# The context's columns of the second block's projection, computed in the two mixtures of experts; a scheduling fence ahead of the recurrence

## The chip, the cores and the metric

One core of a Trainium2 chip runs the whole network in one launch. The metric is the device time of one execution in microseconds (us), taken as the median of several runs. The engines are PE (matrix products), DVE and POOL (elementwise), ACT (activations, copies) and SP (which only starts transfers); ACT and POOL start transfers too. Each engine works off a queue of its own in order.

## The reference

1024 tokens of width 1024 pass two layers, each an attention mixer and a mixture of 16 experts; then a second block takes them together with 256 context tokens `ctx`. In each mixture an expert chooses its 128 best tokens over the whole sequence, so no expert can begin before the scores of all tokens are ranked.

```python
def ec_moe(h, w_router, w_gate, w_up, w_down):
    aff = jax.nn.softmax(jnp.einsum('bsd,de->bse', h, w_router), axis=-1)
    gates, idx = lax.top_k(aff.transpose(0, 2, 1), cap)
    xs = jax.vmap(lambda hb, ib: hb[ib])(h, idx)
    ...
def trunk_layer(x, xc, ...):                      # the second block; xc = ctx
    h = modulate(rmsnorm_2(x, norm1_g), shift1, scale1)
    hc = modulate(rmsnorm_2(xc, norm1_g), modc[0], modc[1])
    q, k, v, rw, gl = jnp.split(h @ w_in, IN_SPLITS, axis=-1)
    qc, kc, vc, rwc, glc = jnp.split(hc @ w_in, IN_SPLITS, axis=-1)
    ya = latent_window_attention(q, k, v, kc, vc, sink)
    ... short_conv(rw), short_conv(rwc), the recurrence over the context's tokens, then over x's
```

Of the context's row of `w_in` only 1952 columns are wanted: keys and values (256) and what the recurrence takes (1696). They depend on `ctx`, `c_ctx` and weights alone, not on the layers before.

## The kernel before

The work runs in stages: even attention with its output projection, mixture 1, odd attention with its output projection, mixture 2, norms and projection of the second block, the recurrence (with the gates' products and the window attention as fill), the merge and the last dense layer. A list scheduler of the language fixes, when the program is built, the order of each engine's queue from the order of the code, priorities and its own idea of durations; at run time an engine never passes its next instruction. Buffers come from rings: `raw` (8) holds loaded weight blocks, `ring` (4 in the mixtures) their two parts.

A float32 product is made of three: each operand is split into a high part (ACT, line 111) and the rest (line 116, on DVE or POOL), `w_h`, `w_l` and `xH`, `xL`, and `passes` lists the three products. In a mixture (`Moe`), the output projection's sink `add` normalises each token tile, `rank` keeps every expert's best (DVE, one `MAX8` and one `MATCH_REPLACE8` after the other), and `choose` ends in `thrb` (lines 682 to 686), the threshold that PE transposes. `gather` then counts places (`oh`), and POOL fetches an expert's tokens (`xs<-h_d,idx`). `gate_up` multiplies them by the expert's first four blocks (48 products of 512 columns); the scheduler has put the splits of expert 0's four blocks ahead of the choice, their low parts on POOL. After an expert POOL adds its tokens to `x_d` (line 805).

In the second block `block2_norms` makes `hH`, `hL` of the tokens and `cH`, `cL` of the context. `Rwkv.project` takes one tile of 128 features after the other through `conv`: two groups of 24 products of 512 columns for the tokens, one of 24 products of 256 columns for the context (`proj_feat`), then the short convolution on DVE. `Window.project` stands between them piece by piece; its tiles 8 and 9 are the context's. Then `R.open` clears tiles and loads constants, and the recurrence's groups take their operands `AR`, `BKf` from DRAM; `others` is the fill (`wK`, `wQ` of the window attention, `ghH`, `ghL`, `gw` of the gates).

Of the kernel before, what the change touches and what calls it, by code (L numbers as in the profile page):

```python
# [23 lines left out]
F32 = mybir.dt.float32  # L24
F32R = mybir.dt.float32r
# [18 lines left out]
class K:  # L44
    """Engines, pools and the few operations that every phase uses."""
# [31 lines left out]
    def banks(s, es, **n):  # L77
        """The eight banks of PSUM, by what they are for, until es closes."""
# [29 lines left out]
    # float32 as the sum of two float32r parts, exact  # L108
# [9 lines left out]
    def row_max(s, pool, todo, mx):  # L118
        """Largest of scores + mask by rows, one column of mx each."""
# [5 lines left out]
    def to_rows(s, pool, cols, n, *dst):  # L125
        """The negatives of columns, one after the other in rows of partition 64."""
# [13 lines left out]
    def weights(s, raw, ring, src, shape, leng=None, queue=None):  # L140
        """A block of weights, loaded and split."""
# [11 lines left out]
    def rstd(s, ss, n, scale, eps, name):  # L153
        """(ss * scale + eps) ** -0.5, few elements per partition."""
# [6 lines left out]
    def bcast(s, pool, ap, n, name, parts=128, **kw):  # L161
        """A row of n values in DRAM on every partition."""
# [5 lines left out]
    def norm_pair(s, pool, xs, gb, outs, eps=EPS, gb2=None):  # L168
        """Two token tiles normalised over their 1024 features and scaled by gb (plus gb2)."""
# [11 lines left out]
    def transpose4(s, src, n=4):  # L181
        """Four [128, 128] blocks of a token tile, transposed into one PSUM bank."""
# [5 lines left out]
    def to_hT(s, src, hH, hL, t):  # L188
        """A token tile [128, 1024] into features by tokens, split."""
# [12 lines left out]
# ---------------------------------------------------------------- even mixer  # L202
# [49 lines left out]
def proj_tile(k, hH, hL, W, t, n):  # L252
    """h of token tile t times a block of weights given in chunks of two k-tiles."""
# [113 lines left out]
NQ = 4  # heads whose operands are on chip at a time  # L367
# [31 lines left out]
def even_head(k, p2, mb, mc, me, h, slot, q_d, k_d, v_d, a_d, r_d):  # L399
# [13 lines left out]
    # values, by tokens shifted by half a tile and by residue classes of 4  # L413
# [2055 lines left out]
```

## Time and profile before

| what | us |
|---|---|
| runs (median of three) | 4460.52 |
| lowest and highest run | 4454.09, 4467.20 |
| span of the profiled execution (no other time of its own is given) | 4467.4 |
| PE busy, share of the span | 3963.4, 89% |
| DVE, ACT, POOL busy | 2938.6, 1815.5, 1109.1 |
| the two longest waits of PE together (line 686, the choice) | 60.2 |

Times in the rows are counted from the first instruction of the profiled execution. A row of the timeline gives start, duration, engine, line, operation, output and inputs, how many were merged, and in brackets how long the engine had been idle and what ended that. Busy shares are averages: PE is at 98% in one stage and at nothing in another.

### The profile page before, as it was taken

The numbers are of one execution on the slowest core, as the hardware profiler recorded it, in microseconds if no ns is written. First come the engines' busy times: TensorE is split into PE (matmuls) and PEld (weight loads), VectorE is DVE, ScalarE is ACT, GpSimd is POOL, SyncE is SP. The second block draws the span as 40 slices with busy tenths as digits, with TensorE's granted clock in tenths as the row PEclk, the third lists the DMA queues.
The fourth block names the chain that finished last, engine by engine and source line by source line (L and its number), as shares of the span: only waits on it lengthen the run. The fifth ranks groups of instructions, "written<-read, shape, count | busy, mean of one in ns | idle before, by whom it ended". The sixth has DMA issues, their size and how long they took to land. (4 is left out here: it accounts for less than half of the span.)

```text
span 4467.4 us, 65652 instructions
## 1 busy us (share of the span) xinstructions
PE 3963.4 (89%) x24208; PEld 3233.3 (72%) x24208; DVE 2938.6 (66%) x5925; ACT 1815.5 (41%) x3066; POOL 1109.1 (25%) x1069
## 2 busy tenths in 40 slices
PE   7898995897978999689948997999988899999998
PEld 7797884775855666567737776777777678888887
DVE  8656658896678875879866793766677565332334
ACT  3223332675447775257634452333333432212212
POOL 2211212121213433112133363222244511101101
PEclk9998997999989999889968998989998999999999
DMA  5758435898267543569933446555756662111112
GB/s 163 228 170 187 110 112 186 304 367 279 82 189 176 116 102 93 188 238 365 329 111 118 148 148 181 138 142 137 166 145 147 190 210 88 57 48 48 49 55 85
DMA packets 568286, 714.12 MB, mean 160 GB/s; under 512 B 243636, under 2 KB 355332, under 8 KB 567964
## 3 DMA queue, kind: packets, MB, share of 16 engines
q1 hardware_dynamic: 467788, 510.50, 37.3%
q0 software_dynamic: 42480, 144.62, 11.9%
q10 hardware_dynamic: 57696, 54.80, 3.8%
q8 instruction: 191, 3.13, 0.3%
q14 instruction: 131, 1.07, 0.1%
HBM read 555.84 MB, written 153.53 MB: 159 GB/s over the span
## 5 line engine op out<-in xcount | busy, mean ns | idle before, releaser
L116 DVE TENSOR_TENSOR w_l<-w_raw,w_h 128x2048 fp32r<-128x2048 f32 (+5 forms) x336 | 592.2, 1769 | 194.1 <-ACT w_h L111 192.9
L111 ACT ACTIVATE w_h<-w_raw 128x2048 fp32r<-128x2048 f32 (+4 forms) x344 | 507.2, 1487 | 437.4 <-PE psO L138 254.5
L138 PE MATMUL psA<-w_h,hH 128*128 128x256 f32 (+3 forms) x896 | 292.6, 330 | 28.9 <-ACT w_h L111 13.7
L138 PE MATMUL psA<-w_l,hH 128*128 128x256 f32 (+3 forms) x896 | 292.6, 327 | 1.9 <-DVE w_l L116 1.7
L138 PE MATMUL psA<-w_h,hL 128*128 128x256 f32 (+3 forms) x896 | 291.3, 326 | 0.0
L116 POOL TENSOR_TENSOR uL<-relu,uH 128x512 fp32r<-128x512 f32 x64 | 82.6, 1291 | 571.9 <-ACT uH L111 571.9
L138 PE MATMUL psA<-w_h,xH 128*128 128x512 f32 x512 | 208.5, 409 | 11.6 <-ACT xH L111 8.8
L138 PE MATMUL psA<-w_l,xH 128*128 128x512 f32 x512 | 211.1, 412 | 7.1 <-DVE w_l L116 6.9
L138 PE MATMUL psA<-w_h,xL 128*128 128x512 f32 x512 | 206.1, 404 | 4.3 <-DVE xL L116 4.3
L138 PEld LDWEIGHTS psA<-w_h,hH 128*128 128x128 f32 x896 | 174.5, 196 | 41.6 <-ACT w_h L111 15.1
L2287 DVE TENSOR_TENSOR relu<-relu 128x512 f32<-128x512 f32 x64 | 44.3, 693 | 238.2 <-ACT relu L2286 238.2
L116 DVE TENSOR_TENSOR PL<-P,PH 128x512 fp32r<-128x512 f32 x192 | 171.1, 903 | 27.3 <-ACT PH L111 27.1
L138 PEld LDWEIGHTS psA<-w_l,hH 128*128 128x128 f32 x896 | 175.3, 196 | 10.4 <-DVE w_l L116 4.6
L138 PE MATMUL psA<-ghH,gwH 128*128 128x256 f32 x512 | 169.6, 331 | 14.5 <-DMA ghH<-hs_d 5.0
L138 PEld LDWEIGHTS psA<-w_h,hL 128*128 128x128 f32 x896 | 175.1, 195 | 5.3 <-issue 2.6
L805 POOL DMA_INDIRECT x_d<-yo,idx x32 | 69.8, 2182 | 421.5 <-ACT yo L804 417.5
L111 ACT ACTIVATE gwH<-gw 128x256 fp32r<-128x256 f32 x256 | 103.3, 414 | 163.1 <-PE psA L138 121.0
L138 PE MATMUL psA<-ghH,gwL 128*128 128x256 f32 x512 | 161.2, 315 | 1.3 <-POOL gwL L116 1.0
L138 PE MATMUL psA<-ghL,gwH 128*128 128x256 f32 x512 | 160.4, 313 | 0.0
L116 POOL TENSOR_TENSOR gwL<-gw,gwH 128x256 fp32r<-128x256 f32 x128 | 97.5, 765 | 248.3 <-ACT gwH L111 207.5
L111 ACT ACTIVATE PH<-P 128x512 fp32r<-128x512 f32 x256 | 154.5, 629 | 6.5 <-POOL PL L116 1.3
L116 POOL TENSOR_TENSOR PL<-P,PH 128x512 fp32r<-128x512 f32 x64 | 90.9, 1420 | 231.2 <-ACT PH L111 178.2
(654 smaller groups left out, 11896.8 us busy)
## 6 DMA issues: line engine op xcount, KB each, us to landing
w_raw<-in_moe_w_gate_dram SPq DMA_DIRECT2D x64, 1024.0 KB
w_raw<-in_moe_w_up_dram SPq DMA_DIRECT2D x64, 1024.0 KB
w_raw<-in_moe_w_down_dram SPq DMA_DIRECT2D x64, 1024.0 KB
gw<-in_w_in_t_dram POOLq DMA_DIRECT2D x64, 512.0 KB, 5.5
wada<-in_w_ada_dram POOLq DMA_DIRECT2D x48, 512.0 KB, 5.8
w_raw<-in_w_mlp_up_dram SPq DMA_DIRECT2D x16, 1024.0 KB
w_raw<-in_w_mlp_down_dram SPq DMA_DIRECT2D x16, 1024.0 KB
AR<-ar_d SPq DMA_DIRECT2D x40, 256.0 KB
```

The source lines that it names most:

```text
L111: s.a.activation(h, x, AF.Copy)
L116: (eng or s.v).tensor_tensor(l, x, f(h), op=ALU.subtract)
L138: s.t.matmul(ps, a, b, start=first and i == 0, stop=last and i == n - 1)
L805: k.g.indirect_dma_start(out=s.x_d[:, :], out_offset=off, in_=y, in_offset=None, compute_op=ALU.add)
L2287: k.v.tensor_tensor(a, a, a, op=ALU.mult)
```

## The change

The context's normalised tokens are made during the even attention and kept in DRAM (`ctx_h`). Each mixture loads four blocks of `w_in` (two chunks of 512 columns), ahead of expert 0's, and `project` multiplies the 256 context tokens by them: 96 products of 512 columns, results to DRAM (`ctx_u`). The splits of expert 0's blocks are written behind that. The second block loads `ctx_u` as `cu` (2 MB), so that norms, splits and 384 products of 256 columns for the context go; `conv` turns a tile of `cu` with two transposes in their place, and the window's tiles 8 and 9 read `cu`. Ahead of `R.open` stands `no_sync_barrier()`, across which the scheduler moves no instruction; it makes nothing wait at run time. Comments and docstrings, which also change, are left out here.

```diff
@@ def even_mixer
     nc, tc = k.nc, k.tc
+    k.ctx = Context(k, w, mod_d)
@@ new class
+class Context:
+    LO, N = 512, 1952
+    CHUNKS = ((512, 1024), (1536, 1952))
...
+    def norms(s):
+        k, w = s.k, s.w
+        with ExitStack() as es:
+            p = k.pool(es, "Rctx", 1)
+            g, ga, x = (p.tile([128, D], F32, name=n) for n in ("cg", "ca", "cx"))
...
+            row(g, w["norm1_g_2"][0])
+            row(ga, s.mod_d[7])
+            k.v.scalar_tensor_tensor(ga, ga, 1.0, g, op0=ALU.add, op1=ALU.mult)
+            row(g, s.mod_d[6])
+            for t in range(2):
+                k.a.dma_start(x, w["ctx_2"][0, 128 * t:128 * t + 128])
+                k.norm_pair(p, [x], ga, [x], gb2=g)
+                k.a.dma_start(s.h_d[t], x)
+    def blocks(s, i):
+        return [s.w["w_in_t"][:, 4 * j:4 * j + 4, lo:lo + 512] for lo in s.CHUNKS[i] for j in range(2)]
+    def project(s, i, p, x, W):
+        k = s.k
+        for c, lo in enumerate(s.CHUNKS[i]):
+            for t in range(2):
+                ps = k.psA()
+                pairs = []
+                for j in range(2):
+                    wh, wl = W[2 * c + j]
+                    for q in range(4):
+                        pairs += passes(x[t][0][:, 4 * j + q], x[t][1][:, 4 * j + q], wh[:, q], wl[:, q])
+                k.mm(ps, pairs)
+                o = p.tile([128, 512], F32, name="th")
+                k.a.activation(o, ps, AF.Copy)
+                a = 2048 - lo if lo == 1952 else 0
+                k.a.dma_start(s.u_d[t][:, lo + a - s.LO:lo + 512 - s.LO], o[:, a:])
@@ class Moe
+        if i == 0:
+            k.ctx.norms()
...
-            split = [k.weights(raw, ring, x, [128, 4, 512], leng=k.g) for x in blocks[:4]]
-            del blocks[:4]
+            first = [k.weights(raw, ring, x, [128, 4, 512], leng=k.g) for x in k.ctx.blocks(i)]
+            split = []
...
-            s.choose()
...
+            def context(t):
+                xs = p.tile([128, D], F32, name="xs", bufs=3)
+                k.d.dma_start(xs, k.ctx.h_d[t])
+                return turned(xs)
+            x = [context(t) for t in range(2)]
+            s.choose()
...
             todo = [s.gather(p, e) for e in range(3)]
+            k.ctx.project(i, p, x, first)
+            split += [k.weights(raw, ring, x, [128, 4, 512], leng=k.g) for x in blocks[:4]]
+            del blocks[:4]
             gu = gate_up(turned(todo[0][0]))
@@ the second block
-        cH = hp.tile([128, 8, TC], F32R, name="cH")
-        cL = hp.tile([128, 8, TC], F32R, name="cL")
+        cu = hp.tile([128, 2, Context.N], F32, name="cu")
+        k.g.dma_start(cu, k.ctx.u_d.rearrange("t p c -> p t c"))
...
             k.banks(es1, Q=1, L0=1, L1=1, P0=1, P1=1)
+            k.tc.no_sync_barrier()
             R.open(es1)
@@ def block2_norms
-        ca = k.bcast(p1, mod_d[7], D, "ca")
-        cs = k.bcast(p1, mod_d[6], D, "cs")
-        k.v.scalar_tensor_tensor(ca, ca, 1.0, g, op0=ALU.add, op1=ALU.mult)
...
-        k.norm_pair(p, xs, ca, xs, gb2=cs)
-        for t in range(2):
-            k.to_hT(xs[t], cH, cL, t)
@@ Window.project
-                ps = proj_tile(k, hH, hL, W, t, 256) if t < 8 else proj_tile(k, cH, cL, W, t - 8, 256)
-                o = p2.tile([128, 256], F32, name="qo")
-                k.a.activation(o, ps, AF.Copy)
+                if t < 8:
+                    ps = proj_tile(k, hH, hL, W, t, 256)
+                    o = p2.tile([128, 256], F32, name="qo")
+                    k.a.activation(o, ps, AF.Copy)
+                else:
+                    o = cu[:, t - 8, 0:256]
@@ Rwkv.project, conv
-                ps = proj_feat(k, cH, cL, W, off, m, slice(0, TC))
+                ps = k.psT()[0:m, :TC]
+                lo = 256 + (128 * tile if tile < 13 else 1600)
+                for t in range(2):
+                    k.t.transpose(ps[:, 128 * t:128 * t + 128], cu[:, t, lo:lo + m], k.ident)
```

**Order on PE at the choice of mixture 1.** In the changed kernel's queue of PE these rows follow each other around the threshold `thrb` (`aff` are the scores, `trib` and `ones` count places):

```order
L138 MATMUL psS<-wr,m_xT 128x16 x8
L692 MATMUL psS<-c_ident,aff 16x128
L745 MATMUL psS<-c_ident,thrb 128x16
L752 LDWEIGHTS trib
L752 MATMUL psO<-sel,trib 128x256
L754 LDWEIGHTS ones
```

Nothing has moved between `aff` and `thrb`: the rows are those of before. Further on, behind the counting for the gathers (`oh`), before's PE goes from the last `oh` straight to expert 0's products (the eight transposes of its tokens `xs` stand four `oh` earlier):

```order
L714 LDWEIGHTS oh
L714 MATMUL psS<-aux,oh 128x5
L138 MATMUL psA<-w_h,xH 128x512
L138 MATMUL psA<-w_l,xH 128x512
L138 MATMUL psA<-w_h,xH 128x512
L138 MATMUL psA<-w_l,xH 128x512
```

In the changed kernel the same place holds the context's products, whose operands bear the same names; `xs` is here the context's second tile:

```order
L773 LDWEIGHTS oh
L773 MATMUL psS<-aux,oh 128x5
L138 MATMUL psA<-w_h,xH 128x512
L138 MATMUL psA<-w_l,xH 128x512
L185 MATMUL psT<-c_ident,xs 128x128 x4
L138 MATMUL psA<-w_h,xL 128x512
L138 MATMUL psA<-w_h,xH 128x512
```

96 products, eight transposes for each context tile and then eight for expert 0 stand there before expert 0's first product; mixture 2 has the same order.

**Order on POOL at the start of the experts.** Before, the four low parts of expert 0's blocks and then five gathers:

```order
L158 TENSOR_TENSOR r_norm<-m_norm,mhalf 128x1 x8
L116 TENSOR_TENSOR w_l<-w_raw,w_h 128x2048 x4
L724 DMA xs<-h_d_5704,idx 128x1024 x5
L805 DMA x_d_72<-yo,idx 1024x1024
L724 DMA xs<-h_d_5704,idx 128x1024
```

In the changed kernel the first four low parts are the context's, and expert 0's stand among the gathers:

```order
L158 TENSOR_TENSOR r_norm<-m_norm,mhalf 128x1 x8
L116 TENSOR_TENSOR w_l<-w_raw,w_h 128x2048 x4
L783 DMA xs<-h_d_5706,idx 128x1024 x3
L116 TENSOR_TENSOR w_l<-w_raw,w_h 128x2048 x3
L783 DMA xs<-h_d_5706,idx 128x1024
L116 TENSOR_TENSOR w_l<-w_raw,w_h 128x2048
L783 DMA xs<-h_d_5706,idx 128x1024
```

So four more low parts of 128x2048 stand on POOL behind the choice.

**Order on POOL at the end of the projection.** Before, POOL goes from the projection's last piece (`bf`) to the fill's loads (masks `mq`, `mk`, keys `wK`, queries `wQ`, `ghH`); the recurrence's clearing comes later:

```order
L1743 TENSOR_TENSOR bf<-kd,E 128x4x64
L1418 DMA mq<-in_c_mask_wq_dram 128x384
L1420 DMA mk<-in_c_mask_wk_dram 128x256
L1424 DMA sk<-in_sink_dram 128x1x1 x2
L1453 MEMSET wKB 1x1280
L1454 MEMSET wVA 128x10
L1456 DMA wK_25935<-wk_d 64x1280 x2
```

Behind the fence the clearing of the recurrence's tiles (`zero`, `XL`, `W`, `Sh`) comes first:

```order
L1807 TENSOR_TENSOR bf<-kd,E 128x4x64
L1836 MEMSET zero 128x260
L1880 MEMSET XL 64x256
L1885 MEMSET W_24949 128x512
L1885 MEMSET W_24950 128x512
L1885 MEMSET Sh_24951 128x512
L1885 MEMSET Sh_24952 128x512
L1479 DMA mq<-in_c_mask_wq_dram 128x384
L1481 DMA mk<-in_c_mask_wk_dram 128x256
```

The fill's loads now stand behind `zero`. On SP the recurrence's first `AR`, `BKf` and `SV` loads now stand ahead of the constants (`dt`, `ms`, `em`, `lnw`, `lnb`) and of the eight `X_d<-zero` stores; before they stood behind them.

## Rows read from the trace of the kernel before

**Rows 1.** Windows at both choices and in mixture 1 (columns: its head).

```profile
core 0: us, PE busy (x) PEld busy (x) DVE busy (x) ACT busy (x) POOL busy (x), PEclk, DMA share, GB/s
720.00:751.00 31.00, 0.41 (x2) 0.12 (x2) 30.07 (x76) 4.26 (x3) 13.50 (x3) 0.50 0.78 292
780.00:820.00 40.00, 30.77 (x121) 23.56 (x120) 25.28 (x18) 19.99 (x18) 0.94 (x1) 0.83 0.63 223
900.00:1000.00 100.00, 98.34 (x484) 77.36 (x483) 94.26 (x130) 73.58 (x61) 23.10 (x10) 1.00 1.05 365
1862.00:1892.00 30.00, 0.38 (x1) 0.09 (x1) 29.49 (x65) 6.24 (x6) 17.97 (x4) 0.51 1.04 392
```

**Rows 2.** Timeline of PE, first choice and expert 0.

```profile
750.98 0.28 PE L686 MATMUL psS<-c_ident,thrb 16*128 16x16 f32 x1 [30.29 <-DVE thrb L684]
764.78 1.95 PE L185 MATMUL psT<-c_ident,xs 128*128 128x128 f32 x8
766.68 0.77 PE L138 MATMUL psA<-w_h,xH 128*128 128x512 f32 x1
770.23 0.40 PE L138 MATMUL psA<-w_h,xH 128*128 128x512 f32 x1
770.46 0.40 PE L138 MATMUL psA<-w_l,xH 128*128 128x512 f32 x1
779.57 1.03 PE L185 MATMUL psT<-c_ident,xs 128*128 128x128 f32 x8
```

**Rows 3.** Timeline of POOL, low parts of expert 0 in the first wait.

```profile
720.74 13.50 POOL L116 TENSOR_TENSOR w_l<-w_raw,w_h 128x2048 fp32r<-128x2048 f32 x3 [2.44 <-PE psS L633]
```

**Rows 4.** Timeline of DVE, the same operation in and behind that stretch.

```profile
721.27 4.14 DVE L677 TENSOR_TENSOR gd<-aff,aux 128x128 f32<-128x128 f32 x1
734.70 0.28 DVE L679 TENSOR_TENSOR gd<-gd,aux 128x128 f32<-128x128 f32 x1
```

**Rows 5.** Windows of the second block's projection and of its end.

```profile
2380.00:2680.00 300.00, 270.18 (x1573) 237.92 (x1572) 243.81 (x414) 147.95 (x324) 146.21 (x102) 0.94 0.43 144
2420.00:2460.00 40.00, 31.31 (x184) 26.80 (x184) 38.89 (x86) 17.59 (x51) 25.22 (x18) 0.91 0.47 159
2460.00:2500.00 40.00, 39.64 (x272) 36.49 (x270) 22.40 (x46) 19.42 (x37) 10.08 (x5) 1.00 0.38 125
2720.00:2760.00 40.00, 27.20 (x134) 22.83 (x135) 14.32 (x41) 9.16 (x26) 15.45 (x26) 0.74 0.73 212
```

**Rows 6.** Windows again, instructions on cH alone.

```profile
2420.00:2460.00 40.00, 6.04 (x32) 4.96 (x32) 0.00 (x0) 0.00 (x0) 0.91 0.47 159
2460.00:2500.00 40.00, 6.17 (x32) 5.10 (x32) 0.00 (x0) 0.00 (x0) 1.00 0.38 125
```

**Rows 7.** Timeline of PE, two of the context's products in a row.

```profile
2673.66 0.28 PE L138 MATMUL psA<-cL,w_h 128*128 128x256 f32 x1
2673.78 0.28 PE L138 MATMUL psA<-cH,w_l 128*128 128x256 f32 x1
```

**Rows 8.** Timeline of DVE and PE, norms of the second block.

```profile
2301.22 2.47 DVE L176 SCALAR_TENSOR_TENSOR xt<-xt,r_norm,ca 128x1024 f32<-128x1024 f32 x2
2334.86 1.11 PE L185 MATMUL psT<-c_ident,xt 128*128 128x128 f32 x4 [5.79 <-DVE cL L116]
```

**Rows 9.** Timeline of ACT's queue, first load of the norms' factors.

```profile
2248.67 0.34 ACTq L165 DMA_DIRECT2D gf<-in_final_norm_dram  x1
```

**Rows 10.** Timeline of POOL, SP and PE, from the projection to the recurrence.

```profile
2682.69 0.91 POOL L1334 DMA_DIRECT2D ghH<-hs_d  x1
2718.45 0.32 POOL L1772 MEMSET zero<- 128x260 f32 x1 [13.93 <-PE psA L138]
2728.49 0.45 SPq L1874 DMA_DIRECT2D AR<-ar_d  x1
2723.99 0.55 PE L138 MATMUL psA<-ghH,gwH 128*128 128x256 f32 x1 [0.23 <-ACT gwH L111]
2750.92 1.22 PE L1890 MATMUL psQ<-AR,BKf 64*128 64x128 f32 x4
```

More of the change, by code (lines that the diff above doesn't have):

```diff
@@ L579, in run, with __init__, row @@
                 sink(t, xt)
+class Context:
+    LO, N = 512, 1952
+    CHUNKS = ((512, 1024), (1536, 1952))
+    def __init__(s, k, w, mod_d):
+        s.k, s.w, s.mod_d = k, w, mod_d
+        s.h_d = k.dram.tile([2, 128, D], F32, name="ctx_h")
+        s.u_d = k.dram.tile([2, 128, s.N], F32, name="ctx_u")
+    def norms(s):
[3 more added lines that the diff above has]
+            g, ga, x = (p.tile([128, D], F32, name=n) for n in ("cg", "ca", "cx"))
+            def row(t, ap):
+                k.a.dma_start(t, bass.AP(tensor=ap.tensor, offset=ap.offset, ap=[[0, 128], [1, D]]))
+            row(g, w["norm1_g_2"][0])
[23 more added lines that the diff above has]
+                k.a.dma_start(s.u_d[t][:, lo + a - s.LO:lo + 512 - s.LO], o[:, a:])
 NE = 16
@@ L1177, in block2 @@
         hL = hp.tile([128, 8, T], F32R, name="hL")
-        cH = hp.tile([128, 8, TC], F32R, name="cH")
-        cL = hp.tile([128, 8, TC], F32R, name="cL")
+        cu = hp.tile([128, 2, Context.N], F32, name="cu")
+        k.g.dma_start(cu, k.ctx.u_d.rearrange("t p c -> p t c"))
         p0 = k.pool(es, "rp0", 1)
-        block2_norms(k, w, x_d, mod_d, hH, hL, cH, cL, rs)
+        block2_norms(k, w, x_d, mod_d, hH, hL, rs)
         R.ranks_weights(p0)
@@ L1196, in stores @@
                     yield
-        more = A.project(es, block, hH, hL, cH, cL)
-        R.project(block, hH, hL, cH, cL, more, stores())
+        more = A.project(es, block, hH, hL, cu)
+        R.project(block, hH, hL, cu, more, stores())
         for _ in more:
@@ L1226, in block2, with block2_norms @@
         merge(k, es, w, ya_d, yr_d, gl_d, x_d, rs, mod_d, out)
-def block2_norms(k, w, x_d, mod_d, hH, hL, cH, cL, rs):
+def block2_norms(k, w, x_d, mod_d, hH, hL, rs):
     with ExitStack() as es:
@@ L1274, in block2_norms @@
                 k.to_hT(h, hH, hL, t)
-        ca = k.bcast(p1, mod_d[7], D, "ca")
-        cs = k.bcast(p1, mod_d[6], D, "cs")
-        k.v.scalar_tensor_tensor(ca, ca, 1.0, g, op0=ALU.add, op1=ALU.mult)
-        xs = []
-        for t in range(2):
-            xt = p.tile([128, D], F32, name="xt", bufs=6)
-            k.d.dma_start(xt, w["ctx_2"][0, 128 * t:128 * t + 128])
-            xs.append(xt)
-        k.norm_pair(p, xs, ca, xs, gb2=cs)
-        for t in range(2):
-            k.to_hT(xs[t], cH, cL, t)
 def proj_feat(k, hH, hL, W, off, m, c):
@@ L1367, in __init__, with project @@
         s.r_d = k.dram.tile([16, 512], F32, name="wr_d")
-    def project(s, es, block, hH, hL, cH, cL):
+    def project(s, es, block, hH, hL, cu):
         k = s.k
@@ L1529, in __init__, with project @@
         s.bon_d = k.dram.tile([128, 8, 8], F32, name="u_bon")
-    def project(s, block, hH, hL, cH, cL, more, stores):
+    def project(s, block, hH, hL, cu, more, stores):
         k, w = s.k, s.w
```

## The prediction

> **What bounds the kernel now.** PE does, stage by stage, with gaps that differ. I read the windows first. In the steady part of a mixture PE is busy 98.3 of 100 us while DVE is busy 94.3 and the DMA engines are full, so three resources end together there and any product that is added costs its whole time. At both choices PE does nothing for some 30 us (0.41 of 31 us, 0.38 of 30 us), and in the first 40 us of expert work it is busy 30.8 [rows 1]. The list of waits and the timeline say what that gap is: PE stands at the transpose of `thrb` for 30.3 us until DVE has ranked [rows 2]. In the projection PE is busy 270 and DVE 244 of 300 us, and the two take turns: 39.6 of 40 us PE in one stretch with DVE at 22.4, then 31.3 PE with DVE at 38.9 [rows 5]. At the passage to the recurrence PE is busy 27.2 of 40 us [rows 5].
>
> So there is a hole of 60 us in which 192 products would be free. Whether they land in it is decided by the order of PE's queue, not by the place in the code.
>
> **The change, part by part.**
>
> *The context's products in the mixtures.* The order shows `thrb` right behind `aff`, as before, and the 96 products behind the counting of the gathers. PE can't reach them before the choice is made; the 30 us stay empty. At the place where they stand nothing is waited for now: expert 0's transposes begin at 764.78 and its products at 766.68 [rows 2]. So expert 0 moves back by the whole block. One product of 512 columns costs 0.23 us (770.23 to 770.46), 96 of them 22.1; sixteen transposes more, at 1.03 for eight, 2.1 [rows 2]. PE starts at the lower of its two clocks behind the wait (granted 0.50 in it, 1.2 GHz [rows 1]; eight transposes take 1.95 at 764.78 and 1.03 at 779.57 [rows 2]), and that is paid once in both kernels. That is 24 us a mixture, and in the steady part nothing gives it back, since PE is at 98%. From below: PE is idle 9.2 of the 40 us after the start [rows 1]; if all of it went, 15 remain. From above: expert 0's low parts, hidden in the wait before, now come on POOL when the ring is free, 4.5 us each (13.50 for three) [rows 3]; two of them show if PE has to wait for them, 33. The loads of the four blocks more replace expert blocks in the same eight raw buffers, and the DMA engines are 37% idle in the stretch behind the start (share 0.63) [rows 1]; I take them at nothing, at most 5. I take 24 twice: **+48** (30 to 66).
>
> *The context's norms* in the even attention: six passes over 1024 columns on DVE at 1.24 (2.47 for two) [rows 8], 7.4 us beside the attention's products; loads on ACT's queue. Nothing to 7.4; no row here says how full DVE is at that place, so I take **+2**, a little under the middle, as part of it must fall beside products.
>
> *The second block's norms.* Five DVE passes (6.2 us) [rows 8], 16 transposes and the wait of 5.8 for `cL` [rows 8] go, and 48 narrow products at 0.12 (5.8) [rows 7]: 17.8 if all lie on the path. The gates' low ranks behind them wait for ACT too, so I take 13 (4 to 18). Against it: `gf` and the other three factors are loaded through ACT's queue at 2248.67 [rows 9], and in the changed kernel two stores of `cu` stand ahead of them there, which need 2 MB landed. At the rate of the second wait, 392 GB/s [rows 1], its 2.0 MB take 5.1 us, so the factors are asked for some 5 to 8 us later; the loads of `x` run beside that. I take +3 (0 to 8). Together **-10** (-18 to +4).
>
> *The projection.* 336 products of 256 columns are left to remove. One costs 0.12 us (2673.66 to 2673.78) [rows 7]. Where they stand matters: the windows on `cH` show 32 (with `cL` 48) in the stretch 2460 to 2500, where PE is full, and as many in 2420 to 2460, where DVE is [rows 5, 6]. Five stretches of the first kind hold 240, three of the second 96. The 240 are worth 28.8 us; the 30 transposes in their place cost 3.9 at 1.03 for eight [rows 2]; the 96 are worth nothing to 11.5, and I take 2, since DVE is busy 38.9 of 40 us there. **-27** (-12 to -36; the small end is a DVE that, at 244 us against PE's 234 left, becomes the bound everywhere).
>
> *The fence.* Before, the fill's loads leave POOL early (`ghH` at 2682.69), and only `zero` waits for PE's last product, to 2718.45; so PE has gate products at 2723.99, while the recurrence's first `AR` is issued at 2728.49 and its first products come at 2750.92 [rows 10]. Now the order is turned: `zero` is ahead of the fill's loads and holds them, and `AR` is ahead of the constants. `AR` can go at about 2719, 9.5 us sooner and no longer among the constants, so the recurrence starts some 10 to 20 us sooner; `ghH`, 1 MB, 5 us at that stretch's 212 GB/s [rows 5], lands behind the clearing and the keys and queries at some 2732 to 2736, so the fill begins 8 to 12 us later. The two nearly cancel on PE, which was idle 12.8 of those 40 us anyway [rows 5]; behind it the recurrence's chain is ahead. I take **-6** (-20 to +10).
>
> Sum: 48 + 2 - 10 - 27 - 6 = +7 us. Against the span of 4467.4 that is 4474.4; that span lies 6.9 above the median of the runs, 4460.52, so I forecast **4467**, 0.2% above it.
>
> **One rule of the Trainium skill speaks against the change.** The row first: an operation of two operands on 128x128 took DVE 4.14 us while POOL made low parts, and the same kind 0.28 us once they were over [rows 3, 4]. The skill's page "SBUF — State Buffer", section "Who interferes with whom", says that a DVE instruction with two inputs in SBUF and a GpSimd instruction that reads SBUF exclude each other for a whole instruction. By that rule the four low parts that are now behind the choice would hold DVE where the experts need it; the trace agrees in the wait itself.
>
> **The rivals.**
>
> *Slower.* POOL's four moved low parts decide: they exclude DVE's own splits at the start of the experts, 4 times about 4 us [rows 4], and expert 0's last block comes late. If half of it reaches PE, each mixture costs 24 + 8 = 32 us, and the sum is +23: 4484. It decides once PE waits over 4 us a mixture for `w_l` or `xL` there. For it: DVE is busy 94% in the steady part [rows 1] and can't catch up. Against it: at the start itself it is busy 25.3 of 40 us [rows 1].
>
> *Faster.* The hidden part of the added products is larger: the start of the experts has 9.2 us of PE idle [rows 1], part of it because splits wait for the ring, and with 22 us of products ahead they may be made meanwhile. At 16 us a mixture, and the norms at their full 17.8 with the factors in time, the sum is 32 + 2 - 17 - 27 - 6 = -16: 4444. Against it: the ring of four blocks is held by the context's blocks until their last products, so little can be made ahead.
>
> *The products run inside the wait after all.* Then the 48 go and the kernel would come to about 4420. It is excluded by the queue order unless PE reaches them before `thrb`.
>
> *The projection doesn't shrink.* With the DVE stretches as bound and only -12, the sum is +22: 4482, the same side as the first rival.
>
> **How the numbers follow.** A measurement of this kernel can tell about 0.3% (13 us, so 4447 to 4474) from no change. The forecast has 0.55 with a range of its own of 4450 to 4484: 0.37 of it lies within 0.3%, 0.13 above, 0.05 below. The two rivals on the slower side have 0.21, all above. The faster one has 0.22, of which 0.03 lies within, and the products inside the wait 0.02. So faster by over 0.3%: 0.26; within: 0.40; slower: 0.34. All terms at their ends together reach farther than is likely at once; the range 4436 to 4496 takes in the cases of both signs and leaves about 2 in 10 outside.
>
> **What would show it.** Right: the wait for `thrb` still near 30 us twice; between it and expert 0's first gate product some 24 us of products on `psA`; the start of expert 0 near 790 instead of 766.7 and the end of mixture 1 as much later. In the projection the PE-full stretches are shorter and the DVE-full ones as long as before. After it the first `psQ` products come sooner after the projection's last product, and `ghH` later. Wrong: the mixtures' ends move by less than 12 us each (the start absorbs them) or by more than 32 (POOL's low parts); the projection shrinks by under 15 or over 36 us; the factors of the norms come so late that the block begins after, not before, its old time; or the recurrence, reordered behind the fence, ends at a time that its start doesn't explain, which I can't read from before's rows.

## The result and the profile after

The changed kernel takes 4488.68 us (median of 4 runs, 4477.74 to 4503.61), the kernel before 4462.15 on the same chip: a ratio of 1.0061, with an interval of 1.0040 to 1.0082. It is slower by 0.6%. That lies in the range of the prediction, but not in the case that was called likeliest; and it lies there partly by luck, since the forecasts of the stages below were off by more, in both directions. On another chip the ratio was 1.0068 (1.0050 to 1.0086).

The profiled execution has a span of 4501.8 us, 34.4 more than before. TensorE's marks (the transposes of `thrb`, the last down product of each mixture, the first product of the first 128-column convolution, the projection's last product, the last product of recurrence and gates, the last of all) divide the difference:

| stretch on TensorE | before, us | after, us | difference | forecast |
|---|---|---|---|---|
| to the first choice (context's norms lie here) | 751.0 | 749.4 | -1.6 | +2 |
| mixture 1, choice to last down product | 352.6 | 364.7 | +12.1 | +24 |
| odd stage and second ranking | 793.5 | 797.6 | +4.1 | 0 |
| mixture 2 | 350.7 | 357.5 | +6.7 | +24 |
| second block's norms and low ranks | 124.4 | 121.0 | -3.4 | -10 |
| projection | 345.9 | 332.9 | -13.0 | -27 |
| recurrence with attention and gates | 839.2 | 866.2 | +27.0 | -6 (fence) |
| rest | 897.3 | 900.2 | +2.9 | 0 |

Here are TensorE's rows at the first choice, which answer to [rows 2]: the wait, the first of the context's products, expert 0's first product.

```profile
749.36 0.28 PE L745 MATMUL psS<-c_ident,thrb 16*128 16x16 f32 x1 [30.28 <-DVE thrb L743]
765.06 0.77 PE L138 MATMUL psA<-w_h,xH 128*128 128x512 f32 x1
792.10 0.50 PE L138 MATMUL psA<-w_h,xH 128*128 128x512 f32 x1 [2.10 <-ACT xH L111]
```

The wait is as long as before, the context's products stand behind it, and expert 0 starts at 792.10 where 766.68 stood. So far all is as forecast. What comes next is in ACT's rows that read the experts' gate products (`th`): experts 0, 1, 3 and 15 (the last) of before, and then of after.

```profile
776.27 0.60 ACT L785 ACTIVATE th<-psA 128x512 f32<-128x512 f32 x1 [2.47 <-PE psA L138]
797.37 0.58 ACT L785 ACTIVATE th<-psA 128x512 f32<-128x512 f32 x1
844.03 0.58 ACT L785 ACTIVATE th<-psA 128x512 f32<-128x512 f32 x1
1086.17 0.57 ACT L785 ACTIVATE th<-psA 128x512 f32<-128x512 f32 x1
```

```profile
799.77 0.60 ACT L853 ACTIVATE th<-psA 128x512 f32<-128x512 f32 x1 [1.89 <-PE psA L138]
813.71 0.60 ACT L853 ACTIVATE th<-psA 128x512 f32<-128x512 f32 x1 [1.04 <-PE psA L138]
850.24 0.58 ACT L853 ACTIVATE th<-psA 128x512 f32<-128x512 f32 x1
1090.40 0.58 ACT L853 ACTIVATE th<-psA 128x512 f32<-128x512 f32 x1
```

Counted from the choice (750.98, 749.36), expert 0 is 25.1 us late, expert 1 18.0, expert 3 7.8, and the last 5.8: most of the added block is given back within three experts. The windows of the first 80 us behind the choice show by what, again before and then after (columns as in [rows 1]).

```profile
751.00:791.00 40.00, 29.76 (x144) 22.62 (x145) 26.49 (x94) 10.09 (x9) 4.98 (x5) 0.67 0.47 158
791.00:831.00 40.00, 33.75 (x149) 26.50 (x147) 25.70 (x23) 25.70 (x22) 1.88 (x1) 0.91 0.68 224
```

```profile
751.00:791.00 40.00, 33.68 (x181) 26.91 (x179) 15.92 (x86) 11.66 (x12) 14.74 (x6) 0.79 0.33 109
791.00:831.00 40.00, 38.58 (x181) 31.30 (x182) 33.48 (x27) 29.45 (x26) 10.52 (x5) 1.00 0.92 327
```

TensorE is busy 72.3 of 80 us instead of 63.5, at a granted clock of 0.79 and 1.00 instead of 0.67 and 0.91: the profile has 362 of its instructions there instead of 293. The start had idle time and slow clock to spare, as the prediction's rival "faster" said, which priced a mixture at 16.

So only 5.8 of the 12.1 us of mixture 1 are there at the last expert's gate products. The rest comes behind them. In before's order the transposes of expert 14's `th` stand among the last expert's products; in the changed order they stand behind all of these, so that TensorE waits for what follows the transposes:

```profile
1095.12 0.79 PE L138 MATMUL psO<-w_h,yH 128*128 128x512 f32 x1 [2.74 <-ACT yH L111]
1099.08 0.80 PE L138 MATMUL psO<-w_h,yL 128*128 128x512 f32 x1 [1.68 <-DVE yL L116]
```

The second profile of the changed kernel and the one without the fence have the same step, of 7.1 and 8.6 us. It is another order by the scheduler at the far end of the mixture, not work that was added.

In the projection, windows of the whole and of two stretches, which answer to [rows 5]:

```profile
2390.00:2723.00 333.00, 276.73 (x1479) 236.65 (x1479) 256.42 (x458) 156.25 (x343) 132.05 (x92) 0.88 0.39 134
2430.00:2470.00 40.00, 30.08 (x151) 25.99 (x150) 39.58 (x78) 15.53 (x43) 24.77 (x20) 0.79 0.55 190
2470.00:2510.00 40.00, 35.38 (x224) 31.58 (x222) 23.27 (x54) 20.14 (x40) 5.15 (x3) 0.94 0.28 90
```

TensorE's busy time fell from 304.5 us (the same stretch of before, 346 us long) to 276.7, but 28 us less work made the stretch only 13 us shorter; VectorE is full in its stretches as before. The clock fell with the work, to 0.79 in the stretch where TensorE waits.

At the passage, which answers to [rows 10], the timelines of POOL, SP, DVE and TensorE show:

```profile
2723.28 0.32 POOL L1836 MEMSET zero<- 128x260 f32 x1 [32.90 <-PE psA L138]
2737.43 0.91 POOL L1392 DMA_DIRECT2D ghH<-hs_d  x1 [3.14 <-DMA sk<-in_sink_dram]
2725.22 0.36 SPq L1938 DMA_DIRECT2D AR<-ar_d  x1
2754.71 8.75 SPq L1874 DMA_DIRECT2D X_d<-zero  x8
2763.51 0.45 SPq L165 DMA_DIRECT2D sb<-in_sink_dram  x1
2767.09 2.80 DVE L1489 TENSOR_SCALAR s<-sb 128x8 f32<-128x8 f32 x1 [38.10 <-DMA sb<-in_sink_dram]
2747.00 0.98 PE L1530 MATMUL psA<-wK,wQ 128*128 128x384 f32 x2 [19.56 <-DMA wQ<-wq_d]
2769.97 0.69 PE L1530 MATMUL psA<-wK,wQ 128*128 128x384 f32 x1 [21.99 <-DVE wmx L1532]
2770.59 1.22 PE L1954 MATMUL psQ<-AR,BKf 64*128 64x128 f32 x4
2771.74 0.58 PE L138 MATMUL psA<-ghH,gwH 128*128 128x256 f32 x1
```

`AR` leaves at 2725.22, 2.2 us behind the projection's last product (2723.06), where 10.3 us were measured before. But this isn't the `AR` that the first product needs. The recurrence runs as two streams, each for half of the heads, and TensorE's order begins with the stream whose loads SP sends last. SP's rows for these, before and then after:

```profile
2734.67 0.99 SPq L1874 DMA_DIRECT2D AR<-ar_d  x2
2736.01 0.36 SPq L1874 DMA_DIRECT2D BKf<-bf_d  x1
```

```profile
2764.00 0.97 SPq L1938 DMA_DIRECT2D AR<-ar_d  x2
2765.01 0.47 SPq L1938 DMA_DIRECT2D BKf<-bf_d  x1
```

By the semaphores in the traces the first `psQ` product waits for this pair in both kernels; the `AR` of 2728.49 in [rows 10] belongs to the other stream. Before, the pair left 16.5 and 17.8 us behind the projection's last product, and now 40.9 and 42.0, behind the constants and the eight `X_d<-zero` stores; it has landed by 2769.35. The sinks' load `sb`, which had landed during the projection before, now stands just ahead of it, at 2763.51. VectorE's `s` waits for it, the row maxima `wmx` stand behind `s`, and the first attention products, which stand ahead of the recurrence on TensorE, wait for those until 2769.97. So two waits end within 1 us of each other. From 2730 to 2760 TensorE is busy for 1 us:

```profile
2730.00:2760.00 30.00, 0.98 (x2) 0.50 (x2) 0.00 (x0) 1.33 (x4) 9.73 (x14) 0.50 1.04 268
```

The DMA engines are full in those 30 us (share 1.04): all loads of the stage start at once.

### The profile page after: what moved, and what is told of

It reads as the page before. It is cut to its first block, busy times and chain, and to the rows that moved or that the text cites. A ratio compares the mean times of both kernels' runs of the same rounds, so it can differ in the third digit from the quotient of the medians.

```text
span 4501.8 us, 65503 instructions
## 1 busy us (share of the span) xinstructions
PE 3947.6 (88%) x24060; PEld 3215.8 (71%) x24060; DVE 2933.2 (65%) x5930; ACT 1837.4 (41%) x3084; POOL 1136.9 (25%) x1079
## 5 line engine op out<-in xcount | busy, mean ns | idle before, releaser
L111 ACT ACTIVATE w_h<-w_raw 128x2048 fp32r<-128x2048 f32 (+3 forms) x352 | 523.0, 1497 | 430.2 <-PE psO L138 254.5
L138 PE MATMUL psA<-w_h,hH 128*128 128x256 f32 (+3 forms) x896 | 297.9, 335 | 25.1 <-ACT w_h L111 12.6
L138 PE MATMUL psA<-w_h,xH 128*128 128x512 f32 x576 | 231.7, 404 | 10.5 <-ACT xH L111 9.0
L138 PE MATMUL psA<-w_l,xH 128*128 128x512 f32 x576 | 232.1, 404 | 4.3 <-DVE w_l L116 4.2
L138 PE MATMUL psA<-w_h,xL 128*128 128x512 f32 x576 | 228.8, 399 | 1.4 <-DVE xL L116 1.2
```

The costliest lines, as they stand in the source:

```text
L111: s.a.activation(h, x, AF.Copy)
L138: s.t.matmul(ps, a, b, start=first and i == 0, stop=last and i == n - 1)
```

## The experiments

All are compared with the kernel before, run on the same chip. The stage is the time from the projection's last product to the last of recurrence and gates. "Left" are the gate products that stand behind the last transposes of the recurrence's output in TensorE's order of instructions. The ratio is of all runs; the columns in us are of one profiled execution each, which in the changed kernel and with the fence alone was the slowest of its runs (4503.61 against a median of 4488.68, 4503.90 against 4493.80), and that of the kernel before is from the first chip.

| kernel | fence | mixtures | projection | busy in the first 60 us | stage | left | ratio |
|---|---|---|---|---|---|---|---|
| before | no | 703.3 | 345.9 | 45.9 | 839.2 | 30 | 1 |
| changed | yes | 722.2 | 332.9 | 15.6 | 866.2 | 22 | 1.0061 (1.0040 to 1.0082) |
| changed again | yes | 716.8 | 330.3 | 17.8 | 878.8 | 22 | 1.0068 (1.0050 to 1.0086) |
| fence only | yes | 702.9 | 331.3 | 15.4 | 884.3 | 144 | 1.0036 (1.0023 to 1.0049) |
| changed, no fence | no | 725.4 | 341.3 | 39.3 | 851.4 | 28 | 1.0060 (1.0031 to 1.0090) |
| sinks early | yes | 718.5 | 332.3 | 12.6 | 939.2 | 261 | 1.0181 (1.0153 to 1.0209) |
| zero early | yes | 722.3 | 332.2 | 13.8 | 886.2 | 142 | 1.0096 (1.0066 to 1.0126) |
| one product | yes | 683.4 | 333.7 | 18.3 | 881.3 | 150 | 1.0027 (1.0004 to 1.0049) |
| no gh loads | yes | 721.6 | 332.3 | 17.6 | 863.0 | 0 | 1.0042 (1.0024 to 1.0061) |
| low parts on GpSimd | yes | 721.3 | 336.5 | 14.8 | 865.4 | 56 | 1.0049 (1.0032 to 1.0065) |
| plus one on ScalarE | yes | 723.1 | 332.6 | 15.0 | 903.8 | 240 | 1.0124 (1.0092 to 1.0156) |
| before, plus one | no | 702.3 | 342.5 | 45.5 | 881.8 | 0 | 1.0050 (1.0030 to 1.0069) |
| no fence, plus one | no | 720.0 | 343.5 | 41.2 | 884.1 | 216 | 1.0122 (1.0086 to 1.0159) |

**The fence alone** (the line added to the kernel before), and **the change without it** (the line taken out).

```
             k.banks(es1, Q=1, L0=1, L1=1, P0=1, P1=1)
+            k.tc.no_sync_barrier()
             R.open(es1)
```

> The kernel before with the fence alone ahead of the recurrence's opening; nothing else changed. Theory A (the fence made the changed kernel slower: it keeps the fill's loads and the one small load of the sinks behind the recurrence's clearing): 25 to 30 us over before, with PE idle some 40 us between the projection's last product and the first products of the recurrence. Theory B (the loss lies in the moved context work, and the late start of the recurrence is only its echo): within 5 us of before.

> The changed kernel without the fence. Theory A: the passage to the recurrence is as in before, and the time is that of the changed kernel less about 30, so 4455 to 4465, level with before: mixtures +19, norms and projection -16. Theory B: no more than 8 us below the changed kernel, 4480 or more.

Measured: 1.0036 for the fence alone, some 16 us, between the two theories. The change without the fence is at 1.0060, as slow as with it. So the theory that the fence is all of the loss fell: each half costs something, and together they cost no more than the second alone. Windows of the first 60 us of the stage and of the rest, before, fence alone, no fence:

```profile
2718.00:2778.00 60.00, 45.91 (x227) 36.85 (x227) 20.36 (x52) 17.28 (x45) 21.79 (x36) 0.76 0.65 185
2778.00:3557.00 779.00, 696.73 (x8157) 560.49 (x8156) 542.63 (x1530) 288.76 (x713) 269.95 (x346) 0.90 0.61 150
```

```profile
2711.00:2771.00 60.00, 15.35 (x83) 12.99 (x81) 11.72 (x29) 6.22 (x17) 24.30 (x41) 0.60 0.84 219
2771.00:3595.00 824.00, 723.36 (x8300) 576.05 (x8298) 550.59 (x1556) 302.17 (x743) 279.23 (x361) 0.89 0.60 147
```

```profile
2733.00:2793.00 60.00, 39.32 (x217) 31.63 (x216) 22.88 (x66) 19.07 (x49) 21.29 (x35) 0.80 0.77 212
2793.00:3584.00 791.00, 695.07 (x8166) 556.66 (x8165) 545.33 (x1531) 288.62 (x713) 271.35 (x347) 0.90 0.60 147
```

The fence takes 30.6 us of TensorE's work out of the first 60 us and gives 14.6 back in the projection, where nothing of the next stage stands any more. The rest of the stage, where the same work is left but for that, has 82 us without TensorE in the kernel before, 101 with the fence alone, 96 without it.

**What holds the passage.** Three edits of the changed kernel: the sinks' load `sb` on GpSimd's queue instead of SP's; the first quarter of the gates' input cleared instead of loaded; the clearing of `X_d` ahead of the second block's norms.

```
-        sb = k.bcast(p1, w["sink_2"][0], 8, "sb")
+        sb = k.bcast(p1, w["sink_2"][0], 8, "sb", eng=k.g)
```

```
         for i, x in enumerate((hH, hL)):
-            k.g.dma_start(f(x), f(h_d[i][:, :, c]))
+            if part == 1:
+                k.v.memset(f(x), 0.0)
+            else:
+                k.g.dma_start(f(x), f(h_d[i][:, :, c]))
```

```
+        with ExitStack() as es0:
+            z = k.pool(es0, "rw4", 1).tile([128, PM // 16], F32, name="zero")
+            k.g.memset(z, 0.0)
+            R.streams = [Stream(R, hs, z) for hs in range(2)]
         block2_norms(k, w, x_d, mod_d, hH, hL, rs)
```

> The changed kernel, fence kept, with the load of the sinks (8 values on all partitions) on POOL's queue with its sister loads in place of SP's, where it stands behind eight stores of zeros. Theory A1 (this one load, for which DVE waits 38 us and PE then 22, is what holds both the fill and the recurrence): 15 to 20 us below the changed kernel, the first products of the recurrence some 20 us sooner. Theory A2 (all loads come late together and fill the DMA engines; the sinks are only the last of them): less than 6 us below it.

> The changed kernel, with the first quarter of the gates' input cleared by VectorE instead of loaded (2 MB fewer of transfers on GpSimd's queue right behind the projection; these gates are wrong). The order of SyncE's queue is as in the changed kernel. Theory B, the passage behind the fence is held by the bytes of all the transfers that the fence lets go together (DMA share 1.03 to 1.05 from 10 to 40 us behind the last product): the sink's load and with it the first product of the recurrence come 6 to 10 us sooner, 38 to 42 us behind the projection's last product (47.5 in the changed kernel). Theory Q, it is held by SyncE's queue, whose 30 issues go out one after the other whatever the others move: 45 to 48 us.

> The changed kernel, with the eight clearing stores of X_d (1.06 MB, 8.75 us of issue on SyncE's queue) put ahead of the second block's norms; the fence stays. By the order of instructions the recurrence's operands of both streams then go out first on SyncE's queue and its products stand first on TensorE. Theory Q, the passage is held by the order of SyncE's queue: the first product of the recurrence 25 to 32 us behind the projection's last product (47.5 in the changed kernel), TensorE busy for 65 us or more of the first 100 us (52.7), and the kernel 8 to 16 us below the changed one. Theory B, by bytes: the 3 MB of operands and what GpSimd's queue moves beside them still fill the transfers, the first product comes 36 us or later, TensorE is busy for less than 60 us of the first 100, and the kernel is 0 to 6 us below the changed one.

With the sinks early the wait for `wmx` falls from 21.99 to 0.34 us, and the one that it had covered shows. TensorE's timeline:

```profile
2745.67 0.69 PE L1530 MATMUL psA<-wK,wQ 128*128 128x384 f32 x1 [0.34 <-DVE wmx L1532]
2767.48 1.19 PE L1954 MATMUL psQ<-AR,BKf 64*128 64x128 f32 x4 [21.12 <-DMA BKf<-bf_d]
```

That `BKf` left at 2762.80, behind the stores of zeros: it is of the pair named above. The recurrence's first product comes 47.7 us behind the projection's last (47.5 in the changed kernel). With the clearing early its operands are first on SP's queue, and it comes after 8.7 us, sooner than either theory said; but then the masks `ms` are late, which VectorE multiplies with its result (`MS`):

```profile
2733.86 1.19 PE L1954 MATMUL psQ<-AR,BKf 64*128 64x128 f32 x4 [4.32 <-DMA BKf<-bf_d]
2744.34 1.19 PE L1954 MATMUL psQ<-AR,BKf 64*128 64x128 f32 x4 [9.28 <-DMA BKf<-bf_d]
2773.76 2.07 PE L1954 MATMUL psQ<-AR,BKf 64*128 64x128 f32 x8 [28.23 <-DVE MS L1956]
```

TensorE works steadily from 48.6 us on. So each time something that stands late on SP's queue ends the passage, at 45 to 49 us. Neither edit made the kernel faster, where the theories gave up to 20 and up to 16 us: the ratios are 1.0181 and 1.0096, both above the changed kernel's, and with the clearing early TensorE is busy for 50.6 of the first 100 us (theory Q said 65 or more). With 2 MB fewer to move the sinks' load leaves 36.6 us behind the projection's last product instead of 40.5 and the first gate product comes at 45.0 instead of 48.7; the recurrence's first product, which by the order then stood behind gate products, came at 50.6. The bytes count, but with half the weight that theory B gave them. Neither theory holds alone: the queue's order decides who waits, and the transfers, all let go together, add to how long. Why SP takes some 40 us to reach the last of these loads was not taken apart.

**The context's products.** One in 24 of them kept.

```
-                k.mm(ps, pairs)
+                k.mm(ps, pairs[:1])
```

> The changed kernel, with one in 24 of the context's products in the two mixtures (their results are wrong; loads, splits, the transposes and the stores stay). Theory P, the mixtures are longer for the products on TensorE: from the threshold's transpose to the last down product the two together take 703 to 708 us (722.2 in the changed kernel, 703.3 before), and the kernel is 14 to 19 us below the changed one. Theory L, they are longer for the 4 MB of weights that each loads more and for the splits on ACT and GpSimd: the two still take 716 us or more, and the kernel stays within 6 us of the changed one.

Measured 1.0027, 0.34 to 0.41 points (15 to 18 us) below the two measurements of the changed kernel (the interval touches that of the first). From the choice the two mixtures take 683.4 us, less than before; but the choice itself came later, as the waits show (38.5 and 38.1 us instead of 30.3 and 29.9):

```profile
PE psS L745 <- DVE thrb L743: 38.5, 1, 38.5
```

Counted from the `aff` transpose ahead of that wait, the two take 760.8 us; 783.1 in the changed kernel, 764.3 before. So theory L fell: the four blocks more of loads and splits cost nothing that shows. The 22.3 us between the two kernels, for what was priced at 48, are not the products' alone, though. With one product in 24 two buffers of the weights' ring come free early, and two of expert 0's four low parts are made in the wait (five low parts behind `aff` there, three in the changed kernel). What the products take, and what it takes that their blocks hold the ring and push expert 0's splits behind the choice, is not separated by this edit.

**The products in the wait.** No fence; the context's tokens loaded into a buffer of the weights' ring and transposed at once, and a scheduling fence behind the context's products, ahead of the choice:

```
+            for t in range(2):
+                k.to_hT(xs[:, t], *s.cT, 0)
+                k.ctx.project(i, p, t, s.cT, first)
+            k.tc.no_sync_barrier()
             s.choose()
```

> The changed kernel without the fence ahead of the recurrence, and with the context's products really inside the two waits: its tokens come through a buffer of the weights' ring, which is free early, and a scheduling fence stands behind its products, ahead of the choice. Theory C (the 24 us of products cost 12 and 7 us because they stood behind the choice): both mixtures take from the threshold on what they take in before, and the time is that without the fence less 15 to 20, so about 4440. Theory D (what the mixtures lost is DMA and POOL work, four more blocks to load and split, and not the products): within 6 us of the kernel without the fence.

Measured 1.0177 (1.0146 to 1.0207), far above what either theory gave. The products do run in the wait, but the choice comes 49.5 and 52.1 us behind `aff` instead of 30.7 and 30.3, and the experts' weights, which had been split in the wait, are split behind it; from `aff` to the last down product a mixture takes 419.0 and 415.9 us (383.3 and 381.0 before). POOL's and DVE's timelines show what the choice waits for:

```profile
722.52 17.96 POOL L116 TENSOR_TENSOR w_l<-w_raw,w_h 128x2048 fp32r<-128x2048 f32 x4 [4.73 <-DMA w_raw<-in_w_in_t_dram]
727.51 8.59 DVE L718 TENSOR_TENSOR sort<-both 16x64 f32<-16x64 f32 x2
742.22 0.33 DVE L718 TENSOR_TENSOR sort<-sort 16x64 f32<-16x64 f32 x2
755.88 0.28 DVE L712 TENSOR_TENSOR both<-sort,new 16x128 f32<-16x128 f32 x1
765.05 0.69 DVE L116 TENSOR_TENSOR cTL<-psT,cTH 128x512 fp32r<-128x512 f32 x1 [8.89 <-ACT cTH L111]
```

Two operations of the ranking take 8.59 us while GpSimd makes low parts, and 0.33 behind them. The rule of the Trainium skill that the prediction cites ("SBUF — State Buffer", section "Who interferes with whom") describes such an exclusion; the trace agrees. But it accounts for a small part: the ranking's last step (`both`) comes 34.5 us behind `aff`, 4.7 later than before. Then VectorE stands for 8.89 us at the low part `cTL` of the second context tile, which the edit's own fence puts ahead of the threshold, and TensorE takes `thrb` only behind the last of the context's products, at 770.88. Behind the choice the low parts of expert 0 fall on the counting of the gathers, where TensorE waits for VectorE's `slot` and `oh` for 25.5 us in mixture 1 (6.0 before). So from the choice on the mixtures take 369.5 and 363.8 us, 16.9 and 13.1 more than before, without one of the context's products there. Whether products that stay out of the threshold's way and leave expert 0's splits in the wait would be free was not tried.

**What sets the projection's length.** The low parts of the second block's weights on GpSimd; then, as GpSimd disturbs VectorE, one addition on ScalarE instead, in the changed kernel, in the kernel before and in the changed one without the fence; and the changed kernel again.

```
-                     [128, 2, n * len(los)], queue=queue) for j in range(4)]
+                     [128, 2, n * len(los)], queue=queue, leng=k.g) for j in range(4)]
```

```
-                k.v.tensor_scalar(l, l, 1.0, None, op0=ALU.add)
+                k.a.activation(l, l, AF.Copy, bias=1.0)
```

> The changed kernel, with the low parts of the second block's projection weights made by GpSimd instead of VectorE (31 instructions, 22.6 us on VectorE in that stretch of the changed kernel). Theory D, the projection of the changed kernel is held by VectorE in every second 40 us stretch (39.6, 39.3 and 38.2 of 40 us, while TensorE stands at 30 to 32), so that products taken away there became idle time: from the first product of the first 128-column convolution to the last product it takes 315 to 325 us (333 in the changed kernel, 332 in the kernel before with the fence alone), and the kernel is 8 to 18 us below the changed one. Theory W, TensorE waits for chains through several engines, not for one that is full: 330 us or more, and no gain or a loss, since GpSimd is 25 to 29 us busy in those same stretches.

> The changed kernel, with the addition of 1 to the decay's tanh (24 instructions, 15.3 us on VectorE in the projection) made by ScalarE, which is busy for 156 of 333 us there. Nothing is put on GpSimd. Theory D, VectorE holds the projection: from the first product of the first 128-column convolution to the last product 318 to 325 us (333 in the changed kernel), and the kernel 6 to 14 us below the changed one. Theory W, TensorE waits there for chains of short steps through ACT and VectorE: a step that goes to ScalarE is no shorter, so 330 us or more.

> The kernel before, with the same addition on ScalarE. Theory D: the projection, which has the context's products still, is held by VectorE in the same stretches (39.3, 38.1 and 38.7 of 40 us), so it takes 331 to 339 us (346 in the kernel before), and unless the recurrence's order gives it back the kernel is 5 to 12 us faster than before. Theory W: 343 us or more, and no gain.

> The changed kernel without the fence, with the same addition on ScalarE. Theory D: the projection takes 326 to 334 us (341 without the fence), and the kernel stands 6 to 14 us below the one without the fence; still above the kernel before by 5 to 20 us, for the 22 us of the context's products in the mixtures. Theory W: 338 us or more.

> The changed kernel once more, on the chip of the last three: the measure for them. If its profile holds what was read from the first one, the two mixtures together take 718 to 726 us from the threshold's transpose to the last down product, the projection 331 to 335 us, the first product of the recurrence comes 46 to 49 us behind the projection's last, and the kernel is 0.4 to 0.9% above the kernel before.

Theory D's times came nowhere: 336.5 us with the low parts on GpSimd, and 332.6, 342.5 and 343.5 with the addition on ScalarE, where 332.9, 345.9 and 341.3 stood (342.5 is just under theory W's bound). The changed kernel again held what was read from its first profile within 1.2 us of the bounds given, but for its stage, 12.6 us longer. In the first, VectorE didn't even become emptier. DVE's groups in the projection, changed kernel and then this one:

```profile
L1785 DVE TENSOR_TENSOR_SCAN F<-reset,l 128x256 f32<-128x256 f32 x40 | 34.0, 882 | 0.4
L1808 DVE SCALAR_TENSOR_TENSOR ta<-ta,nk 128x512 f32<-128x512 f32 x16 | 16.5, 1032 | 3.1 <-POOL kd L1805 3.1
```

```profile
L1785 DVE TENSOR_TENSOR_SCAN F<-reset,l 128x256 f32<-128x256 f32 x40 | 37.0, 955 | 0.3
L1808 DVE SCALAR_TENSOR_TENSOR ta<-ta,nk 128x512 f32<-128x512 f32 x16 | 19.2, 1201 | 1.1 <-POOL kd L1805 1.1
```

The same instructions are 8 and 16% longer beside 31 more on GpSimd. With the addition on ScalarE VectorE is emptier (windows of the projection: 248.95 us, from 256.42), and the length stays. But in the stretch where VectorE was full it is full still:

```profile
2391.00:2724.00 333.00, 277.71 (x1479) 237.46 (x1479) 248.95 (x433) 168.52 (x366) 129.62 (x92) 0.87 0.39 134
2432.00:2472.00 40.00, 30.90 (x149) 25.79 (x148) 39.70 (x83) 17.46 (x50) 25.89 (x19) 0.79 0.54 190
```

So these edits do not rule out that VectorE, beside a GpSimd that is busy for 25 of these 40 us, holds such stretches.

One number stands nearly still: the last of the 24 operands `bf` that VectorE writes comes 298.8 us behind the first 128-column product in the kernel before, 299.2 with the fence alone, 301.7 in the changed kernel, 303.5 and 306.0 with the low parts on GpSimd and the addition on ScalarE. None of these edits shortens it. That fits a chain of steps through several engines, one feature block after the other, but which chain was not tried.

The kernel before, with that one addition moved, is 0.50% slower: its projection is 3.4 us shorter and its stage 42.6 us longer, though nothing in that stage was edited (9.3 us of this come back behind it, since the merge's first products stand in it).

## Why the prediction was right or wrong

**The total** came out 28 us above the sum of +7 in the profiled executions, because the errors partly cancel: some -29 in the mixtures, +14 in the projection, +33 at the fence, +10 in the rest. The range held it; the sum behind it did not.

**Where the products stand: right.** Both waits stayed at 30 us, and expert 0 began at 792 (forecast 790).

**What they cost: the mechanism right, the size wrong.** The step was "in the steady part nothing gives it back". 48 us were forecast, 18.8 and 13.4 measured in the two profiles of the changed kernel (12.1 and 6.7 us a mixture, 11.3 and 2.2 in the second). The delay of 25 us is there at expert 0 and has shrunk to 8 by expert 3. The lower bound, 15 a mixture from 9.2 us of idle time in 40, counted one stretch of the start only; over the first 80 us TensorE stood idle for 16.5 us, of which 7.7 are left, and the granted clock there is higher (0.79 and 1.00, from 0.67 and 0.91). Half of mixture 1's loss comes from the order at its end, which the prediction did not look at.

**Context's norms** (+2): nothing shows, the choice came 1.6 us sooner. **The second block's norms** (-10): -3.4, and -2.4 without the fence, in the range given. The block's first transposes come 3.5 us later behind the mixture than before, the sign of the late factors that the prediction priced at 3.

**The projection: wrong.** The step was "the 240 are worth 28.8 us", since they stand in stretches where TensorE is full (by stretches of 20 us it is 216 of the 336). The products went, and TensorE's busy time with them (28 us), but not the time: -13.0 in all, of which the fence alone makes -14.6, and -4.6 without the fence. With the fence in both, the stretch takes 331.3 us with the context's products and 332.9 without them. The rows fit a TensorE that is full because the work comes to it in lumps, and that with less to do waited for the same next lump; what sets the pace of the lumps stays open. The rival "the projection doesn't shrink" was right in the length. Its reason, VectorE as the bound, is neither shown nor refuted.

**The fence: wrong.** The step was "the two nearly cancel": recurrence 10 to 20 us sooner, fill 8 to 12 later. Measured from the projection's last product the recurrence starts after 47.5 us (32.7 before) and the gate products after 48.7 (5.8 before). The prediction took the first `AR` on SP's queue for the operand of the recurrence's first product. That `AR` did go early, but the first product needs the pair of the other stream, which the new order leaves behind the constants and the stores of zeros: it left 24 us later than before, counted from the projection's last product. The prediction also followed `zero` and `ghH` and not the small loads whose results stand first in another engine's queue: `sb` is late on SP's queue, and VectorE, then TensorE, stand in order behind it. And it left out that what had been spread over the projection's end now fills the DMA engines for 30 us. The gain in the projection (14.6) was not foreseen.

**The last warning came true.** The prediction named a recurrence that "ends at a time that its start doesn't explain" as a way to be wrong. The stage holds the same work in every kernel of the table and takes 839 to 939 us, and the kernel before has the shortest of all. An addition moved ahead of it made it 42.6 us longer. The longest stages, 939, 904, 886, 884 and 884, have 261, 240, 142, 144 and 216 gate products left behind the recurrence, which then had nothing to fill its waits with; the shortest, 839 to 866, have 0 to 56. But 879 and 882 us with 22 and 0 left show that this isn't all, and two profiles of the changed kernel differ by 13 us. So part of what the change and the fence "cost" is the loss of an order that happened to be good: shown for the addition, likely but not separated for the change itself. Whether the products left behind cause the longer stage was not tried.

**The rivals.** "Slower" gave 4484, near the measured time, by a mechanism that didn't happen: TensorE's waits for `w_l` in the first mixture are 4.0 us in all (6.1 before), and the mixtures grew by less than forecast, not by more. That number was right by accident. No kernel that was tried beats the one before.

## What to carry to other kernels

A stretch in which an engine is full doesn't mean that work taken from it shortens the stretch: look at how regular the next engine's last result is, and ask what that waits for. Ahead of a fence, list every load that it holds back, down to the smallest, with its place on its queue and who stands in order behind its reader, and find out which of several like loads the first product waits for; removing one such wait only uncovers the next while the transfers are full. And where a scheduler orders the code, measure a harmless edit as well: here one that moved 24 instructions to an engine with room cost 0.5%, nearly as much as the change.

## What was not expected of the hardware

Low parts made by GpSimd in the wait for the choice set its length. With three of them (13.49 us) the choice came 30.3 us behind TensorE's last transpose. With five (22.55 us, in the kernel with one product in 24) it came after 38.5, for on VectorE an operation that takes 0.28 us behind the low parts [rows 4] took 4.21 beside them, and two of the ranking 4.65 together. An engine that seems free in a wait is not free if it slows the engine waited for.
